# A two-layer hybrid decoder trunk: Strassen pair products with other weight loads, other DMA sums and a written order on every engine

## The chip, the cores and the metric

The kernel runs on one core of one Trainium2 chip. The metric is the device time of one execution in microseconds, as a median over runs. One execution is also profiled; its trace gives the rows that are quoted here. Engines are named as in the profile: PE (TensorE), PEld (its weight loads), DVE (VectorE), ACT (ScalarE), POOL (GpSimd) and SP (SyncE, which here only issues DMAs).

## What is computed

Two layers over a sequence of 1024 tokens of width 1024. Cut to what matters:

```python
for l in range(2):
    shift, scale, gate = split(silu(c) @ w_ada[l] + b_ada[l], 3)
    h = rmsnorm(x, norm_g[l]) * (1 + scale) + shift
    p = h @ w_in[l]                       # 1024 x 9224, split into head groups
    mq, mk, mv, mo, mz, mi, mf, rq, rk, rv, rz = split_cols(p)
    qk = silu(causal_dwconv(concat(mq, mk), conv_w[l], conv_b[l]))      # 4 taps
    cell = mlstm_chunkwise(qk, mv, mi + b_igate[l], mf + b_fgate[l])    # 4 heads x 256
    y_m = sigmoid(mo) * head_layernorm(cell, gn_m[l]) * silu(mz)
    ret = retention_chunkwise(rotary(rq), rotary(rk), rv)               # 4 heads x 256
    y_r = head_layernorm(ret, gn_r[l]) * silu(rz)
    x = x + gate * (concat(y_m, y_r) @ w_out[l])
return rmsnorm(x, final_g)
```

Both head groups are causal linear attentions. The kernel computes them in four chunks of 256 tokens with a running state.

## The kernel before

Every large product is made in three matmuls of float32r pieces (`mm3`, lines 153 to 156): an operand is split into a rounded high part H and the rest L, and HH + HL + LH is summed in PSUM. So each weight tile of 128 x 512 that comes from DRAM is cast by ACT (`wH`) and subtracted by DVE or POOL (`wL = w - wH`, `split_to`, line 758).

**Stages of a layer.** First come the normalised transposed input `hT` and three columns of gates, then `build_forms` (line 570), then the *pair stage* with the projections and the attention, then the output projection (`out_units`). The pair stage is most of the time.

**Pairs.** Two blocks of 128 columns of `w_in` (or two heads' value columns) are multiplied with both halves of the sequence by a Strassen-Winograd scheme: seven products in place of eight. `build_forms` makes the sums of the input (U1 to U4) once per layer, on DVE. `weight_forms` (line 601) makes the seven forms of four weight blocks a11, a12, a21, a22 (a *quad*): a11, a12, a22 and the sums S1 to S4. A job of `pair_units` (line 662) is one quad: seven products of twelve 128x512 matmuls into banks X, Y and Z, where X and Z are added to again after ACT has copied an intermediate sum out of them (`A.copy(keep[n], bank)`, line 674). DVE adds the copies (lines 677 to 684). A job of `vpair_units` (line 690) takes two quads, seven products in two halves (`part`) of 24 matmuls of 256 columns; line 720 is its copy. `plan` (line 1450) lists a layer's 32 jobs: 4 of values (v), 8 of q, 8 of k, 4 of z gates (z) and 8 of a z and an o gate (a).

**The weights before.** Of the seven forms of a quad, a12 and a22 go through `loaded` (line 615): POOL issues a plain load into `wH` (L617), ACT writes its negative into `wL` (L618), and POOL issues an adding DMA of the same block into `wL` (L619). The others start from three tiles that SP loads (`raw`, L607), three adding DMAs of POOL (L623, L632, L633) and one DVE sum (L627), then a cast and a subtraction each (L759, L760). The `Feeder` (line 649) keeps five forms ready (`AHEAD`).

**What follows a product.** `conv_silu` (line 762) is a chain ACT, six small DVE steps, ACT, DVE for the four-tap convolution and its SiLU (L766 to L776); `spill` (line 809) splits the result and stores it to DRAM. `rot_done` does the rotary form, `z_done` and `zo_done` the gates, `store` (line 693) the values. All of a chain is written at the product that it follows.

**Attention.** `attention` (line 862) is a generator that is launched after a head's k job; each `yield n` lets n products pass. Several heads may be under way. It loads q, k, values and key rows back from DRAM, makes scores, state updates and outputs for four chunks, normalises, and stores to `ndr`.

**Order.** PE's instructions stand as written (`manual`, line 1281). The orders of ACT, DVE, POOL and SP are made by a list scheduler from priorities, except in the startup; lines 671 and 717 raise the priority of what follows a product. Each engine, once built, runs its own list strictly in order, and so does SP with its DMAs. Tiles come from tagged pools; a new tile waits until a buffer of its tag is free. Tags here: `acc` (6 buffers), `th` (4), `raw` (5), `wH` and `wL` (5 each), `b` (61).

Of the kernel before, what the change touches and what calls it, by code (L numbers as in the profile page):

```python
# [36 lines left out]
NB = 61  # L37
NACC = 6
NTH = 4
NW = 5  # L40
NRAW = 5
AHEAD = 4
# [47 lines left out]
def tile_hybrid_trunk(ctx, tc, x, xt, c, positions, w_ada, b_ada, norm_g, w_in, w_blk, w_val, conv_w, conv_b,  # L90
# [38 lines left out]
    def launch(gen, delay=0):  # L129
        uid[0] += 1  # L130
        pending.append([clock[0] + delay, uid[0], gen])

    def tick():
        clock[0] += 1
        while True:
            due = [p for p in pending if p[0] <= clock[0]]
            if not due:
                return
            p = min(due, key=lambda q: (q[0], q[1]))
            try:  # L140
                p[0] = clock[0] + next(p[2])
            except StopIteration:
                pending.remove(p)

# [8 lines left out]
    def mm3(o, lt, rt, start, stop, more=False):  # L153
# [29 lines left out]
           for l in range(DEPTH)]  # L183
    mdr = [dpool.tile([NH, T], F32, name=f"mdr{l}") for l in range(DEPTH)]
# [90 lines left out]
    def ada_rows(l, c0, accs):  # L275
        acc = wt("acc", 512, NACC)
        accs.append(acc)
        prev = None
        for k in range(KT + 1):
            raw = None  # L280
            if k < KT:
                raw = wt("acc", 512, NACC)
                Q.dma_start(raw, w_ada[l, k * P:(k + 1) * P, c0:c0 + 512])
            if k == 1:
                V.tensor_scalar(acc, prev, cact[:, 0:1], None, ALU.mult)
            elif k > 1:
                V.scalar_tensor_tensor(acc, prev, cact[:, k - 1:k], acc, ALU.mult, ALU.add)
            prev = raw
            yield 2

    def ada_columns_later(l):
        for half in range(2):
            accs = []
            for which in range(2):
                yield from ada_rows(l, which * D + half * 512, accs)
            yield 2
            pt = ps_a()
            for which in range(2):
                for i in range(4):
                    PE.matmul(pt[:, which * 4 + i:which * 4 + i + 1], accs[which][:, i * P:(i + 1) * P], ones,  # L300
                              start=True, stop=True)
            finish_gsh(l, half * 4, 4, pt[:, 0:4], pt[:, 4:8])
            yield 1

    def gate_rows(l, res):
        for half in range(2):
            accs = []
            yield from ada_rows(l, 2 * D + half * 512, accs)
            brow = wt("th", 512, NTH)
# [5 lines left out]
            a2 = (wt("wH", 512, NW, F32R), wt("wL", 512, NW, F32R))  # L315
# [5 lines left out]
            g = bt()  # L321
            V.tensor_copy(g, pt)
            res.append(g)
# [38 lines left out]
    def load_w_raw(l, c0):  # L362
        for p in range(2):
            raw = wt("raw", 512, NRAW)
            Q.dma_start(raw, w_block(l, c0, p))
            yield raw

    def split_w(raw, eng=G, tiles=None):
        wH, wL = tiles or (wt("wH", 512, NW, F32R), wt("wL", 512, NW, F32R))
        split_to((wH, wL), raw, eng)  # L370
        return [(wH[:, a * P:(a + 1) * P], wL[:, a * P:(a + 1) * P]) for a in range(4)]

    def third(pair, p):
        return [t[:, p * 512:(p + 1) * 512] for t in pair]

    def load_w(l, c0):
        res = []
        for raw in load_w_raw(l, c0):
            res += split_w(raw)
        return res  # L380
# [16 lines left out]
    def rotary_tables():  # L397
        c1, c2, c3 = two_pi_split()
        t0, t1 = wt("q", 1024, 2), wt("kc", 1024, 1)
        ang, turn, tmp, rnd = (t0[:, i * CH:(i + 1) * CH] for i in range(4))  # L400
        a1, pos = (t1[:, i * CH:(i + 1) * CH] for i in range(2))
        a2 = ang
        for n in range(4):
            i, cs = n // 2, slice((n % 2) * CH, (n % 2 + 1) * CH)
            Q.dma_start(pos.bitcast(I32), positions[0:1, n * CH:(n + 1) * CH].to_broadcast([P, CH]))
            yield 2
            V.tensor_copy(ang, pos.bitcast(I32))
            V.tensor_scalar(ang, ang, kc[:, C_FREQ:C_FREQ + 1], None, ALU.mult)
# [4 lines left out]
            V.scalar_tensor_tensor(turn, a2, c2, turn, ALU.mult, ALU.add)  # L413
            for src, cc in ((a1, c2), (a2, c1), (a1, c1)):
# [13 lines left out]
            yield 2  # L428
# [113 lines left out]
    def gate_z(src, g, sign=1.0):  # L542
        th = wt("th", 512, NTH)
        A.activation(th, src, AF.Tanh, scale=0.5 * sign)
        V.scalar_tensor_tensor(g, th, 1.0, src, ALU.add, ALU.mult)

    def gate_o(src, g, store, sign=1.0):
        th = wt("th", 512, NTH)
# [21 lines left out]
    def build_forms(hT):  # L570
        F = {"11": [hT[k][0] for k in range(4)], "21": [hT[k][0] for k in range(4, 8)],
             "22": [hT[k][1] for k in range(4, 8)], "U1": [], "U2": [], "U3": [], "U4": []}
# [11 lines left out]
        for k in range(4):  # L584
# [8 lines left out]
            u4 = whole(hT[k + 4][0])  # L593
            V.scalar_tensor_tensor(u4, u2, -1.0, u4, ALU.mult, ALU.subtract)
            keep("U4", u4)
        return F

    ORDER = (("X", "11"), ("Y", "21"), ("X", "U2"), ("Z", "U1"), ("X", "U3"), ("Z", "22"), ("X", "U4"))
    VORDER = (("Y", "21"), ("X", "11"), ("X", "U2"), ("Z", "U1"), ("X", "U3"), ("Z", "22"), ("X", "U4"))

    def weight_forms(blk, first):
        def tiles():
            return wt("wH", 512, NW, F32R), wt("wL", 512, NW, F32R)

        def raw(src):
            t = wt("raw", 512, NRAW)
            Q.dma_start(t, src)  # L607
            return t

        def split(r, eng):  # L610
            w = tiles()
            split_to(w, r, eng)
            return w

        def loaded(src):
            w = tiles()
            G.dma_start(w[0], src)  # L617
            A.activation(w[1], f(w[0]), AF.Copy, scale=-1.0)  # L618
            G.dma_start(w[1], src, accum_op=ALU.add)  # L619
            return w  # L620

        a, s1, s3 = raw(blk[0][0]), raw(blk[1][0]), raw(blk[0][0])
        G.dma_start(s1, blk[1][1], accum_op=ALU.add)  # L623
        if first == "21":
            yield loaded(blk[0][1])
        w = split(a, G)
        V.tensor_tensor(a, a, s1, ALU.add)  # L627
        yield w
        if first == "11":
            yield loaded(blk[0][1])  # L630
        w = split(a, V)
        G.dma_start(a, blk[0][1], accum_op=ALU.add)  # L632
        G.dma_start(s3, blk[1][0], accum_op=ALU.add)  # L633
        yield w
        yield split(s1, G)
        yield split(s3, V)
        yield split(a, G)
        yield loaded(blk[1][1])

    def pair_forms(l, cols2):  # L640
        for w in weight_forms([[w_block(l, c, kh) for kh in range(2)] for c in cols2], "11"):
            yield [(w[0][:, k * P:(k + 1) * P], w[1][:, k * P:(k + 1) * P]) for k in range(4)]

    def vpair_forms(l, heads):
        gens = [weight_forms([[w_val[l, h, kh * 2 + kp] for kh in range(2)] for h in heads], "21") for kp in range(2)]
        for ws in zip(*gens):
            yield [(w[0][:, a * HD:(a + 1) * HD], w[1][:, a * HD:(a + 1) * HD]) for w in ws for a in range(2)]

    class Feeder:
        def __init__(self, gens):  # L650
            self.gens, self.ready = gens, []
            self.forms = (w for g in gens for w in g())

        def take(self):
            while len(self.ready) <= AHEAD:
                w = next(self.forms, None)
                if w is None:
                    break
                self.ready.append(w)
            return self.ready.pop(0)  # L660

    def pair_units(feed, F, done, loose=False):
        bank, keep = {}, {}
        for n, (b, form) in enumerate(ORDER):
            w = feed.take()
# [24 lines left out]
    def vpair_units(l, feed, F, heads):  # L690
        banks, keeps = [{}, {}], [{}, {}]

        def store(part, i, half, src):
            vH, vL = (wt("acc", 512, NACC, F32R) for _ in range(2))
            A.activation(vH, src, AF.Copy, scale=-1.0 if i else 1.0)
            if i:
                V.scalar_tensor_tensor(vL, src, -1.0, f(vH), ALU.mult, ALU.subtract)
            else:
                V.tensor_tensor(vL, src, f(vH), ALU.subtract)
            dst = vdr[l][heads[i]][half * 2 + part].rearrange("(i t p) c -> i p t c", i=2, p=P)  # L700
# [3 lines left out]
        for n, (b, form) in enumerate(VORDER):  # L704
            w = feed.take()
            for part in range(2):
                bank, keep = banks[part], keeps[part]
# [9 lines left out]
                with tc.high_priority():  # L717
                    if n == 1:
# [3 lines left out]
                        store(part, 0, 0, bank["Y"])  # L722
# [3 lines left out]
                    elif n == 4:  # L726
                        V.tensor_tensor(keep[3], bank["X"], keep[3], ALU.add)
                        store(part, 1, 1, keep[3])
                    elif n == 5:
                        V.tensor_tensor(bank["Z"], bank["Z"], keep[2], ALU.add)  # L730
                        store(part, 0, 1, bank["Z"])
                    elif n == 6:
                        store(part, 1, 0, bank["X"])
                yield

    def z_done(store):
        def done(m, half, src):
            g = wt("acc", 512, NACC)
            gate_z(src, g, -1.0 if m else 1.0)
            Q.dma_start(store[m][half], g)  # L740
        return done

    def zo_done(store):
        g, late = {}, []

        def done(o, half, src):
            if not o:
                g[half] = wt("acc", 512, NACC)
                gate_z(src, g[half])
                if half:  # L750
                    gate_o(late[0], g[1], store[1], -1.0)
            elif half:
                late.append(src)
            else:
                gate_o(src, g[0], store[0], -1.0)
# [6 lines left out]
    def conv_silu(l, hg, which, m, half, pt, halo):  # L762
# [4 lines left out]
        if half == 0:  # L767
            V.tensor_copy(halo, pt[:, HALF - 3:HALF])
        for d in range(1, 4):
# [4 lines left out]
        th = wt("th", 512, NTH)  # L774
        A.activation(th, acc, AF.Tanh, scale=0.5)
        V.scalar_tensor_tensor(acc, th, 1.0, acc, ALU.add, ALU.mult)  # L776
        return acc

    def k_store(src, l, hg, m, half):
        zt = wt("th", 512, NTH)  # L780
# [773 lines left out]
```

## Time and profile before

| what | value |
|---|---|
| median of 2 runs | 2927.63 us (2924.39 to 2930.87) |
| the profiled execution | 2911.5 us |
| its span, first to last instruction | 2909.8 us |
| mean granted TensorE clock | 0.888 |
| busy: PE, DVE, POOL, ACT | 2279.8, 1677.8, 1151.3, 1142.9 us |
| DMA moved | 567.91 MB, mean 195 GB/s |

An engine's busy time is the union of its instructions' spans. Matmuls are pipelined and their spans overlap, so a busy PE is not a PE at its peak; its pace is read from the distances of starts. The granted clock is the share of full clock that PE was given. The DMA share is the mean busy share of the core's 16 DMA engines. In a row of waits, "A <- B" means that A's engine sat idle until B ended; a wait for several things is put down to the one that came last.

### The profile page before, as it was taken

The page shows a single profiled execution, that of the slowest core. Times are in us where ns is not written, and L with a number is a line of the kernel's source. Part 1 is how long each engine was busy: PE and PEld are TensorE (multiplying, and loading weights), DVE is VectorE, ACT ScalarE, POOL GpSimd, SP SyncE. Part 2 cuts the span into 40 slices and gives each one's busy share as a digit, 9 for nine tenths or more (in the row PEclk, how much of TensorE's full clock was granted, in tenths as well). Part 3 has the DMA queues.
Part 4 walks back from the last instruction along what each step waited for, and adds up shares of the span by engine and source line. Part 5 has one row for each costly group of instructions (what it writes and reads, how often), then busy time and mean ns, then how long its engine had stood idle before and what let it go on. Part 6 is the DMA issues. An engine that isn't in the chain of part 4 may idle for free. (4 is left out here: it accounts for less than half of the span.)

```text
span 2909.8 us, 35824 instructions
## 1 busy us (share of the span) xinstructions
PE 2279.8 (78%) x11483; PEld 1931.8 (66%) x11483; DVE 1677.8 (58%) x3073; ACT 1142.9 (39%) x2091; POOL 1151.3 (40%) x1174
## 2 busy tenths in 40 slices
PE   4878787768777767689998788788777776777998
PEld 3668666657565755577776677667766575666777
DVE  4875365655655556656638556456455556574744
ACT  4523233233434344444354333333344434353433
POOL 0533454444434343422266344255343434343123
PEclk7978898888898888799998898889888888898999
DMA  6277787878777877768542787688777787776766
GB/s 212 52 169 199 180 222 199 228 215 240 203 208 186 225 205 186 196 172 275 199 141 62 184 223 210 175 231 230 211 205 184 190 223 184 193 203 171 237 209 170
DMA packets 532553, 567.91 MB, mean 195 GB/s; under 512 B 196466, under 2 KB 347770, under 8 KB 532364
## 3 DMA queue, kind: packets, MB, share of 16 engines
q1 hardware_dynamic: 463676, 440.55, 48.3%
q0 software_dynamic: 68544, 124.81, 24.0%
q8 instruction: 90, 1.47, 0.2%
q14 instruction: 99, 0.81, 0.1%
q10 hardware_dynamic: 144, 0.26, 0.0%
HBM read 409.20 MB, written 156.27 MB: 194 GB/s over the span
## 5 line engine op out<-in xcount | busy, mean ns | idle before, releaser
L154 PE MATMUL pp<-b,wH 128*128 128x512 f32 x1616 | 681.6, 422 | 338.1 <-ACT acc L674 326.0
L156 PE MATMUL pp<-b,wL 128*128 128x512 f32 x1616 | 664.8, 411 | 13.3 <-DMA wL<-in_w_blk_dram 8.0
L155 PE MATMUL pp<-b,wH 128*128 128x512 f32 x1616 | 668.0, 413 | 4.3 <-DVE b L1120 4.3
L154 PEld LDWEIGHTS pp<-b,wH 128*128 128x128 f32 x1616 | 327.1, 202 | 431.2 <-ACT acc L674 351.2
L760 POOL TENSOR_TENSOR wL<-raw,wH 128x512 fp32r<-128x512 f32 x276 | 392.0, 1433 | 405.4 <-ACT wH L759 332.2
L759 ACT CAST wH<-raw 128x512 fp32r<-128x512 f32 x476 | 289.7, 616 | 372.0 <-PE pp L155 129.8
L156 PEld LDWEIGHTS pp<-b,wL 128*128 128x128 f32 x1616 | 326.3, 202 | 90.2 <-DMA wL<-in_w_blk_dram 9.3
L155 PE MATMUL pp<-wL,b 128*128 128x256 f32 (+1 forms) x1024 | 325.2, 318 | 64.5 <-DMA wL<-in_w_val_dram 57.7
L155 PEld LDWEIGHTS pp<-b,wH 128*128 128x128 f32 x1616 | 328.5, 203 | 70.1 <-DVE b L1120 6.5
L154 PE MATMUL pp<-wH,b 128*128 128x256 f32 (+1 forms) x1024 | 325.7, 318 | 55.4 <-ACT acc L720 24.5
L156 PE MATMUL pp<-wH,b 128*128 128x256 f32 (+1 forms) x1024 | 321.8, 314 | 0.2
L155 PEld LDWEIGHTS pp<-wL,b 128*128 128x128 f32 x1024 | 215.3, 210 | 74.3 <-DMA wL<-in_w_val_dram 61.0
L154 PEld LDWEIGHTS pp<-wH,b 128*128 128x128 f32 x1024 | 215.0, 210 | 66.6 <-ACT acc L720 25.8
L618 ACT ACTIVATE wL<-wH 128x512 fp32r<-128x512 f32 x136 | 85.7, 630 | 430.2 <-DMA wH<-in_w_blk_dram 288.8
L760 POOL TENSOR_TENSOR acc<-acc,acc 128x512 fp32r<-128x512 f32 x128 | 179.7, 1420 | 156.4 <-ACT acc L759 126.0
L619 POOL DMA_DIRECT2D wL<-in_w_blk_dram x104 | 92.0, 884 | 343.1 <-ACT wL L618 260.4
L760 DVE TENSOR_TENSOR wL<-raw,wH 128x512 fp32r<-128x512 f32 x200 | 156.7, 785 | 111.6 <-ACT wH L759 111.1
L156 PEld LDWEIGHTS pp<-wH,b 128*128 128x128 f32 x1024 | 214.9, 210 | 7.3 <-DVE b L1120 2.4
L771 DVE SCALAR_TENSOR_TENSOR acc<-pp,cols,acc 128x511 f32<-128x511 f32 (+2 forms) x192 | 142.4, 742 | 33.4 <-ACT acc L766 32.1
L627 DVE TENSOR_TENSOR raw<-raw,raw 128x512 f32<-128x512 f32 x68 | 54.8, 807 | 147.7 <-POOL wL L760 104.2
L759 ACT CAST acc<-acc 128x512 fp32r<-128x512 f32 x128 | 78.4, 617 | 130.7 <-DVE acc L848 48.3
L760 POOL TENSOR_TENSOR sL<-th,sH 128x384 fp32r<-128x384 f32 (+1 forms) x64 | 62.3, 973 | 108.9 <-ACT sH L759 87.8
(342 smaller groups left out, 4393.1 us busy)
## 6 DMA issues: line engine op xcount, KB each, us to landing
raw<-in_w_blk_dram SPq DMA_DIRECT2D x171, 256.0 KB
raw<-in_w_blk_dram POOLq DMA_DIRECT2D x156, 256.0 KB, 5.3
vdr<-acc SPq DMA_DIRECT2D x128, 256.0 KB
ring<-vdr SPq DMA_DIRECT2D x64, 512.0 KB
qdr<-acc SPq DMA_DIRECT2D x128, 256.0 KB
q<-qdr SPq DMA_DIRECT2D x64, 512.0 KB
kfr<-acc SPq DMA_DIRECT2D x128, 256.0 KB
kc<-kfr SPq DMA_DIRECT2D x64, 512.0 KB
```

The costliest lines, as they stand in the source:

```text
L154: PE.matmul(o, lt[0], rt[0], start=start, stop=False, skip_group_check=more)
L155: PE.matmul(o, lt[0], rt[1], start=False, stop=False, skip_group_check=more)
L156: PE.matmul(o, lt[1], rt[0], start=False, stop=stop, skip_group_check=more)
L618: A.activation(w[1], f(w[0]), AF.Copy, scale=-1.0)
L619: G.dma_start(w[1], src, accum_op=ALU.add)
L627: V.tensor_tensor(a, a, s1, ALU.add)
L759: A.copy(dst[0], src)
L760: eng.tensor_tensor(dst[1], src, f(dst[0]), ALU.subtract)
L771: V.scalar_tensor_tensor(acc[:, d:], pt[:, 0:HALF - d], wcol, acc[:, d:], ALU.mult, ALU.add)
```

## The change

- **Weights.** All seven forms of a quad are made alike. SP loads seven tiles from the ring `R` (13 buffers, which replaces `raw` and `wL`); four adding DMAs of POOL make S1 = a21 + a22, S2 = a11 + S1, S4 = a12 + S2 and S3 = a21 + a11, of which S2 and S4 add a tile of SBUF. ACT casts each, and POOL (a12, S3, a22) or DVE (a11, S2, S1, S4) subtracts. `loaded` and the DVE sum go.
- **Times.** The `Feeder` holds a list of events. Each event has the number of the product at which its instruction is written: loads 6 to 11 products ahead of use in a pair job, casts 3, subtractions 2.
- **One-product steps.** Chains are generators whose links stand one product apart.
- **Attention.** One head at a time follows `TABLE`, one entry per product; the next may begin after entry 23. Loading of key rows (`k_load`) and their split (`k_split`) are apart.
- **Order.** From `build_forms` to the last gate pair every engine and the load queue run as written. Outside, the scheduler uses another model of time (`schedule_with_timeline_sim`). Layer 0's plan and layer 1's are reordered. `th` is merged into `acc` (11 buffers); `b` has 59. The sums U4 are made after the others. The gate rows of the second layer go through DRAM (`gbd`).

```diff
-NB = 61
-NACC = 6
-NTH = 4
+NB = 59
+NACC = 11
 NW = 5
-NRAW = 5
-AHEAD = 4
+NR = 13
...
-    def weight_forms(blk, first):
...
-        def loaded(src):
-            w = tiles()
-            G.dma_start(w[0], src)
-            A.activation(w[1], f(w[0]), AF.Copy, scale=-1.0)
-            G.dma_start(w[1], src, accum_op=ALU.add)
-            return w
...
+    def ring_load(src):
+        r = wt("R", 512, NR)
+        Q.dma_start(r, src)
+        return r
+
+    def high(r, h=None):
+        h = wt("wH", 512, NW, F32R) if h is None else h
+        A.copy(h, r)
+        return h
+
+    def low(h, r, eng=G):
+        lo = wt("R", 512, NR, F32R)
+        eng.tensor_tensor(lo, r, f(h), ALU.subtract)
+        return lo
...
+    POOL_LOW = ("a12", "S3", "a22")
...
+        def quad(self, names, blk, t0, u):
+            r, h = {}, {}
+            at = {n: t0 + u * i for i, n in enumerate(names)}
...
+            def add(n, src):
+                G.dma_start(r[n], r[src] if isinstance(src, str) else src, accum_op=ALU.add)
...
+            T2 = at["S2"]
+            ev(T2 - 10, load, "S1", a21)
+            ev(T2 - 8, load, "S2", a11)
+            ev(T2 - 8, add, "S1", a22)
+            ev(T2 - 6, load, "S4", a12)
+            ev(T2 - 6, add, "S2", "S1")
+            ev(T2 - 4, add, "S4", "S2")
+            T4 = at["S3"]
+            ev(T4 - 7, load, "S3", a21)
+            ev(T4 - 5, add, "S3", a11)
+            for n, src in (("a11", a11), ("a12", a12), ("a22", a22)):
+                ev(at[n] - 7 + u, load, n, src)
+            for n in names:
+                ev(at[n] - 4 + u, hi, n)
+                ev(at[n] - 2, lo, n, G if n in POOL_LOW else V)
...
+    def conv_chain(l, hg, which, m, half, pt, halo):
...
         A.activation(acc, pt, AF.Identity, bias=cl[:, 8 + ct:9 + ct], scale=cl[:, 72 + ct:73 + ct])
...
+        yield 1
         for d in range(1, 4):
...
+        yield 1
+        th = wt("acc", 512, NACC)
         A.activation(th, acc, AF.Tanh, scale=0.5)
+        yield 1
         V.scalar_tensor_tensor(acc, th, 1.0, acc, ALU.add, ALU.mult)
+        yield 1
+        yield from spill(acc, l, hg, which, m, half)
...
+    TABLE = ("q0 k0 v0 d0 d1 t0", "", "", "m0", "s0 S0", "k1", "m1 q1", "v1", "V001", "S1 t1", "U01",
+             "k2 q2 d2", "s1 v2", "V10 U2 m2", "S2", "k3 d3", "V11 U3", "t2 q3", "s2 v3", "", "V20 U4 m3", "S3", "",
+             "V21 U5", "", "", "", "V30", "V31", "")
+    RELEASE = 23
...
+        jobs_manual = tc.manual_schedule()
+        jobs_manual.__enter__()
+        launch(build_forms(hT, F))
...
-                    launch(attention(l, h, gt), 4)
+                    launch(attention(l, h, gt), 6, 1)
+        jobs_manual.__exit__(None, None, None)
...
-    with tile.TileContext(nc) as tc:
+    with tile.TileContext(nc, schedule_with_timeline_sim=True) as tc:
```

464 lines of the change are left out of this document (251 added, 213 removed).

## The prediction

> **What bounds it now.** I read the windows by stage first, then who PE waits for, then the timeline of one long wait. The page gives the span; the other rows are busy us (instructions) of PE, PEld, DVE, ACT and POOL, then granted clock, DMA share and GB/s, for pairs, output projection, pairs, output projection of the two layers, and then the same for the attention's PSUM tiles `pa` alone.
>
> ```profile
> span 2909.8 us, 35824 instructions
> ```
>
> ```profile
> 119.00:1306.00 1187.00, 889.80 (x4654) 763.42 (x4653) 711.13 (x1349) 437.86 (x816) 484.22 (x509) 0.87 0.75 198
> 1306.00:1556.00 250.00, 240.18 (x1042) 191.65 (x1043) 130.79 (x197) 113.17 (x184) 106.20 (x84) 0.98 0.59 190
> 1556.00:2706.00 1150.00, 887.25 (x4632) 766.36 (x4630) 661.06 (x1213) 444.09 (x827) 487.10 (x511) 0.87 0.75 196
> 2706.00:2910.00 204.00, 184.45 (x805) 150.13 (x804) 103.80 (x178) 80.04 (x144) 50.82 (x43) 0.96 0.68 205
> ```
>
> ```profile
> 119.00:1306.00 1187.00, 161.05 (x1124) 152.29 (x1124) 75.89 (x187) 35.06 (x77) 0.87 0.75 198
> 1556.00:2706.00 1150.00, 157.85 (x1080) 149.50 (x1080) 75.68 (x182) 36.40 (x79) 0.87 0.75 196
> ```
>
> In the output projections PE is busy 240 of 250 us; in the pair stages 890 of 1187 and 887 of 1150. These two stages are the change's ground. Busy spans overlap, so the pace is read from starts in the timeline:
>
> ```profile
> 706.63 0.39 PE L154 MATMUL pp<-b,wH 128*128 128x512 f32 x1
> 709.35 0.39 PE L154 MATMUL pp<-b,wH 128*128 128x512 f32 x1
> 713.56 0.28 PE L155 MATMUL pa<-q,kc 128*128 128x256 f32 x1
> 713.68 0.28 PE L156 MATMUL pa<-q,kc 128*128 128x256 f32 x1
> ```
>
> The first two rows are twelve matmuls apart, one Strassen product: 2.72 us. A 256-column matmul takes 0.12 us, so half a value product (24 of them) takes 2.88. By the plan a layer has 28 jobs of 7 products and 4 value jobs of 14 halves: 196 x 2.72 + 56 x 2.88 = 694 us. With 1124 and 1080 attention matmuls of 0.12 (135 and 130 us), PE needs 829 and 824 us. It takes 1187 and 1150, so 684 us are lost. The waits of PE (us in total, times, longest) say to whom:
>
> ```profile
> PE pp L154 <- ACT acc L674: 326.0, 54, 17.7
> PE pp L155 <- DMA wL<-in_w_val_dram: 57.7, 15, 8.1
> PE pp L154 <- ACT acc L720: 24.5, 5, 13.3
> PE pp L156 <- DMA wL<-in_w_blk_dram: 8.0, 3, 4.3
> ```
>
> L674 is ACT's copy of bank X, 0.58 us long, after which PE may add to X again. It is late because ACT is one queue, and other work stands ahead of the copy:
>
> ```profile
> 1104.60 0.63 ACT L618 ACTIVATE wL<-wH 128x512 fp32r<-128x512 f32 x1 [4.02 <-DMA wH<-in_w_blk_dram]
> 1109.50 0.63 ACT L775 ACTIVATE th<-acc 128x512 f32<-128x512 f32 x1 [3.08 <-DVE acc L773]
> 1111.46 0.58 ACT L674 COPY acc<-pp 128x512 f32<-128x512 f32 x1
> ```
>
> ```profile
> 1099.08 0.85 POOL L617 DMA_DIRECT2D wH<-in_w_blk_dram  x1
> ```
>
> ```profile
> 1112.09 0.79 PE L154 MATMUL pp<-b,wH 128*128 128x512 f32 x1 [14.00 <-ACT acc L674]
> ```
>
> ACT stood 4.02 us for a weight whose load POOL had issued 5.5 us earlier, and 3.08 us for the convolution on DVE, with the copy behind both; PE stood 14.00 us. Then its matmul took 0.79 us where a warm one takes 0.39. So a wait of this length is paid twice.
>
> [...]
>
> **The change, part by part.** The groups and issues concerned (count | busy us, mean ns | idle before them), then the DMA queues (packets, MB, share of 16 engines) and the landing of POOL's loads to `raw` and to `wL`:
>
> ```profile
> L618 ACT ACTIVATE wL<-wH 128x512 fp32r<-128x512 f32 x136 | 85.7, 630 | 430.2 <-DMA wH<-in_w_blk_dram 288.8 <-DMA wH<-in_w_val_dram 107.0 <-issue 22.1
> L759 ACT CAST wH<-raw 128x512 fp32r<-128x512 f32 x476 | 289.7, 616 | 372.0 <-PE pp L155 129.8 <-DMA raw<-in_w_blk_dram 58.1 <-PE pp L156 43.0
> L760 DVE TENSOR_TENSOR wL<-raw,wH 128x512 fp32r<-128x512 f32 x200 | 156.7, 785 | 111.6 <-ACT wH L759 111.1
> L627 DVE TENSOR_TENSOR raw<-raw,raw 128x512 f32<-128x512 f32 x68 | 54.8, 807 | 147.7 <-POOL wL L760 104.2 <-issue 23.7 <-DMA raw<-in_w_blk_dram 12.3
> L619 POOL DMA_DIRECT2D wL<-in_w_blk_dram x104 | 92.0, 884 | 343.1 <-ACT wL L618 260.4 <-ACT cf L969 36.2 <-ACT b L806 9.4
> L617 POOL DMA_DIRECT2D wH<-in_w_blk_dram x104 | 69.6, 669 | 33.0 <-PE pp L156 30.5 <-issue 2.5
> ```
>
> ```profile
> q1 hardware_dynamic: 463676, 440.55, 48.3%
> q0 software_dynamic: 68544, 124.81, 24.0%
> raw<-in_w_blk_dram POOLq DMA_DIRECT2D x156, 256.0 KB, 5.3
> DMA to landing us min/median/max: 3.7/4.6/8.4
> ```
>
> Work is counted per quad, the seven forms of four weight blocks: 72 of them (28 + 2 x 4 per layer). *ACT:* seven copies of 0.62 to 0.63 us before and after, change 0. What goes is standing in its queue for `wH`, 288.8 + 107.0 = 396 us: a plain load now leaves SP three products (8.2 us) before ACT's copy needs it. *DVE:* two subtractions and one sum (2 x 0.785 + 0.807 = 2.38 us) become four subtractions (3.14): 0.76 x 72 = 55 us more, 27 per layer beside 711. I cost it at nothing, since DVE would be busy (711 + 27) / 1012 = 73% of the stage forecast below; uncovered it is 55 us. *POOL:* seven DMA issues become four, three fewer at 0.67 to 0.88 us, 2.0 to 2.6 us a quad, off the path. *SP:* three loads become seven; one issue takes about 0.4 us:
>
> ```profile
> 1098.99 0.38 SPq L607 DMA_DIRECT2D raw<-in_w_blk_dram  x1
> ```
>
> That is 4 x 72 x 0.38 = 109 us in a queue that holds the stores of `spill`, `store` and `finish` and the attention's loads; nothing, while SP is ahead. *DMA engines:* q0 took 24.0% of 2909.8 us for 124.81 MB, 476 transfers of 256 KB, 1.47 us each; q1 takes 48.3% for 440.55 MB, 0.84 us per 256 KB. Of POOL's seven, two are plain; at 0.84 us these leave (7 x 1.47 - 2 x 0.84) / 5 = 1.72 us for an adding one. Before: 5 x 1.72 + 5 x 0.84 = 12.8 us a quad. After: 4 x 1.72 + 7 x 0.84 = 12.8. If adding costs only 1.47, it is 11.8 against 12.8, 72 us less in all. The two adds whose source lies in SBUF have no row here; if each costs a plain transfer more, 2 x 0.84 x 72 = 121 us come on top. I take 0, by the rows of adds from DRAM, and keep -72 and +121.
>
> *Order.* Where the scheduler ordered ACT, DVE, POOL and SP, each now runs as written, links of a chain one product apart. A link of 0.6 to 0.8 us has 2.72 us to finish before the next engine reaches its successor, so the 3.08 us kind of standing goes too. The moved attention issues per head, on SP, 4 loads each of q, k and values, 12 of key rows and 16 stores, past weight loads written up to ten products ahead. Its last head starts some 22 products before the pair stage ends and its table has 30, so about a quarter of its 135 / 8 = 17 us of PE, 4 us a layer, goes over into the output projection: moved, not added, and taken as 0. The price is that nothing overtakes: behind a late weight ACT holds the bank copies and DVE's chains wait. `build_forms` only spreads; its DVE work stays. `schedule_with_timeline_sim` touches the output projections, idle 250 - 240 + 204 - 184 = 30 us: at best 30 us; at worst they fall to the pair stage's busy share 0.75, 240 / 0.75 - 250 + 184 / 0.75 - 204 = 111 us. I take 0, their own rows.
>
> *Sum.* The pair stages hold 1187 x 0.75 = 890 and 1150 x 0.75 = 863 us of full DMA use, more than PE's 829 and 824, so once ACT's standing is gone the transfers are late next. How dense can they run?
>
> ```profile
> 400.00:700.00 300.00, 226.22 (x1066) 186.61 (x1065) 181.08 (x336) 98.19 (x186) 131.42 (x135) 0.89 0.80 216
> 1910.00:1970.00 60.00, 51.77 (x229) 41.85 (x229) 30.74 (x54) 20.01 (x37) 31.55 (x32) 0.93 0.89 234
> ```
>
> The best 60 us hold 0.89. I take 0.88 for the whole stage: 890 / 0.88 = 1012 and 863 / 0.88 = 980 us, 175 and 170 saved. Against the waits it fits: 345 of the 416 us in the four rows above and their cold clock. The profiled execution took 2911.5 us: 2911.5 - 345 = 2566. The median of the runs shown, 2927.63, is 16 above it, so the forecast is 2582 us. Its own range goes from a share of 0.95 (937 + 908, 492 saved: 2436) to 0.80 (1113 + 1078, 146 saved: 2782), which also holds the DMA bounds (-72 / 0.88 = -82 and +121 / 0.88 = +138: 2500 and 2720).
>
> **Rivals.** *Slower: POOL's chained adds.* S1 must land before S2 adds it, S2 before S4, and S3 after its load, each with two products, 5.44 us. Landing from a POOL issue now has a median of 5.3 us for `raw` and of 4.6 for `wL`, with a maximum of 8.4, at a share of 0.75. While POOL stands, the low parts of three products, of the spills and of the scores wait behind, and then PE. With three such waits a quad, a landing of L costs 72 x 3 x (L - 5.44) us: from L = 7.0 the 345 us are gone; at 7.5, 445 us, 3027. For it: denser DMAs land later. Against: forms are finished one to three products before use.
>
> *Transfers stay at their present best.* If 0.80, the best 300 us, is a ceiling, 2782. For it: 300 us hold nearly half a stage's jobs of every kind. Against: the 0.89 row. [...]
>
> *All stalls go.* DMA at 0.95, PE near 829 / 937 = 88%: 2436.
>
> *The wait only moves.* `acc` has 11 buffers and now serves `th` too, and with a product between links a convolution's tile lives some seven products. ACT's first instruction then waits for a store to land, with the copies behind it: the 326.0 us stay, the 57.7 + 8.0 of DMA waits go, 2862, 2930 if they return elsewhere, and over 2% slower only if the ring starves the casts too. For it: a k job alone fills 8 to 9 buffers. Against: only the 8 k jobs of a layer are such, and 4 of them have no convolution.
>
> **Chances.** Forecast 0.43, all stalls go 0.14, transfers capped 0.15, the wait moves 0.12, POOL's adds 0.16. Faster by over 2% (about what a measurement of this kernel can tell from no change) is 0.43 + 0.14 + 0.15 = 0.72; of the moved wait 0.09 is within 2% and 0.03 slower; slower 0.16 + 0.03 = 0.19. The range runs from 2410, leaving out a little of the all-go case (0.05), to 2915, leaving out POOL's adds (0.15 of 0.16).
>
> **What would show it.** Right: the wait on L674's successor falls from 326 us to under 100; no ACT idle ended by a load of `wH`; pair stages near 1010 and 980 us at a DMA share of 0.88 and a clock over 0.92; output projections as now. Wrong: POOL idle ended by landings of its own adds, with PE waiting for POOL's low parts (first rival); a share stuck at 0.80 with SP or ACT waiting for landings (second); ACT idle ended by landings of stores from `acc` (fourth). What would break the prediction is a longer output projection, or SP standing for a store with weight loads queued behind it: then every engine waits and the DMA share falls below 0.75.

## Result and profile after

The changed kernel takes 2621.97 us (median of 2 runs, 2620.6 to 2623.33) against 2927.63: ratio 0.8956, 95% interval 0.8909 to 0.9003, faster. The forecast was 2582. The profiled execution took 2620.6 us, 291 less than that of before (2911.5).

First the page of the changed kernel: its span, and the rows of the DMA queues (packets, MB, share of 16 engines).

```profile
span 2618.9 us, 35874 instructions
...
q1 hardware_dynamic: 503420, 512.92, 61.7%
q0 software_dynamic: 39168, 71.32, 16.2%
```

Then the windows by stage, cut at the same places in PE's program as before: pairs and output projection of the first layer, then of the second (busy us and instructions of PE, PEld, DVE, ACT, POOL; granted clock, DMA share, GB/s).

```profile
117.00:1106.00 989.00, 853.40 (x4628) 739.30 (x4627) 743.98 (x1374) 417.11 (x808) 429.18 (x415) 0.93 0.88 248
1106.00:1404.00 298.00, 258.64 (x1091) 205.22 (x1089) 141.60 (x224) 124.23 (x201) 107.51 (x81) 0.91 0.46 153
1404.00:2398.00 994.00, 858.83 (x4634) 741.93 (x4632) 695.82 (x1270) 425.70 (x822) 433.67 (x420) 0.93 0.85 239
2398.00:2619.00 221.00, 188.26 (x782) 150.84 (x780) 102.05 (x164) 77.19 (x138) 49.88 (x41) 0.93 0.65 191
```

For a fair difference the kernel before is cut at the same places in its program, by the trace at 119, 1302, 1561 and 2706 us:

```profile
119.00:1302.00 1183.00, 889.68 (x4654) 763.42 (x4653) 708.69 (x1346) 435.89 (x813) 483.21 (x508) 0.87 0.75 198
1302.00:1561.00 259.00, 245.30 (x1065) 195.79 (x1065) 137.38 (x205) 119.54 (x195) 111.26 (x87) 0.97 0.58 187
1561.00:2706.00 1145.00, 882.25 (x4610) 762.22 (x4608) 656.91 (x1207) 439.68 (x820) 483.05 (x510) 0.87 0.76 197
2706.00:2910.00 204.00, 184.45 (x805) 150.13 (x804) 103.80 (x178) 80.04 (x144) 50.82 (x43) 0.96 0.68 205
```

The two pair stages lost 194 and 151 us, together 345; the two output projections gained 39 and 17, together 56; the startup lost 2. That is the whole difference of 291. Who PE waits for in the changed kernel (us, times, longest):

```profile
PE pa L1082 <- DVE cL L1055: 75.7, 37, 5.4
PE pp L155 <- ACT wH L381: 58.8, 8, 21.1
PE pp L155 <- ACT acc L716: 32.9, 17, 5.3
PE pp L155 <- ACT b L1213: 29.3, 6, 8.8
```

L716 is the old L674, the copy of bank X: 326.0 us have become 32.9. ACT now comes to this copy early: 73 of its 156 times it stood ready until PE's product ended (142.3 us in all), before 9 times (9.8 us). New at the top is the low part `cL` of the attention's state, which DVE makes one product behind ACT's high part. POOL does stand for the landings of what its adds need:

```profile
POOL R L661 <- DMA R<-in_w_blk_dram: 135.5, 40, 11.7
POOL R L661 <- DMA R<-R: 59.3, 18, 6.1
```

### The profile page after: what moved, and what is told of

It reads as the page before. It is cut to its first block, busy times and chain, and to the rows that moved or that the text cites. A ratio compares the mean times of both kernels' runs of the same rounds, so it can differ in the third digit from the quotient of the medians.

```text
span 2618.9 us, 35874 instructions
## 1 busy us (share of the span) xinstructions
PE 2239.9 (86%) x11483; PEld 1898.4 (72%) x11483; DVE 1752.9 (67%) x3165; ACT 1110.6 (42%) x2087; POOL 1041.1 (40%) x978
## 3 DMA queue, kind: packets, MB, share of 16 engines
q1 hardware_dynamic: 503420, 512.92, 61.7%
q0 software_dynamic: 39168, 71.32, 16.2%
## 5 line engine op out<-in xcount | busy, mean ns | idle before, releaser
L155 PE MATMUL pp<-b,wH 128*128 128x512 f32 x1616 | 660.9, 409 | 72.6 <-ACT acc L716 32.9
L157 PE MATMUL pp<-b,R 128*128 128x512 f32 x1616 | 658.7, 408 | 39.0 <-POOL R L386 28.7
L386 POOL TENSOR_TENSOR R<-R,wH 128x512 fp32r<-128x512 f32 x276 | 410.9, 1495 | 314.5 <-ACT wH L381 286.7
L381 ACT CAST wH<-R 128x512 fp32r<-128x512 f32 x616 | 373.1, 617 | 360.7 <-DMA R<-in_w_blk_dram 78.6
L155 PEld LDWEIGHTS pp<-b,wH 128*128 128x128 f32 x1616 | 320.1, 198 | 146.7 <-ACT acc L716 42.3
L157 PEld LDWEIGHTS pp<-b,R 128*128 128x128 f32 x1616 | 318.2, 197 | 126.1 <-POOL R L386 39.6
L386 DVE TENSOR_TENSOR R<-R,wH 128x512 fp32r<-128x512 f32 x340 | 269.9, 801 | 141.4 <-ACT wH L381 134.6
L156 PE MATMUL pp<-R,b 128*128 128x256 f32 (+1 forms) x1024 | 319.6, 312 | 27.4 <-POOL R L386 24.3
L156 PEld LDWEIGHTS pp<-R,b 128*128 128x128 f32 x1024 | 208.2, 203 | 38.6 <-POOL R L386 27.1
L661 POOL DMA_DIRECT2D R<-R x136 | 121.3, 898 | 247.2 <-DMA R<-in_w_blk_dram 88.0
L716 ACT COPY acc<-pp 128x512 f32<-128x512 f32 x156 | 91.4, 586 | 150.7 <-PE pp L157 142.3
L661 POOL DMA_DIRECT2D R<-in_w_blk_dram x104 | 100.8, 969 | 82.1 <-DMA R<-in_w_blk_dram 47.5
```

The lines of the kernel that those rows point to most:

```text
L155: PE.matmul(o, lt[0], rt[0], start=start, stop=False, skip_group_check=more)
L156: PE.matmul(o, lt[0], rt[1], start=False, stop=False, skip_group_check=more)
L157: PE.matmul(o, lt[1], rt[0], start=False, stop=stop, skip_group_check=more)
L381: A.copy(h, r)
L386: eng.tensor_tensor(lo, r, f(h), ALU.subtract)
L661: G.dma_start(r[n], r[src] if isinstance(src, str) else src, accum_op=ALU.add)
```

## Experiments

All ratios are against the kernel before on the same chip, with their 95% intervals. The median of that kernel was 2912.79 to 2918.31 us there. So the changed kernel's gain of 0.1044 is about 305 us, and 0.01 is 29 us.

The change has three parts that can be separated: the code of the pair stage (weight loads, chained sums, one-product links, longer rings, the attention's table, the jobs in another order), the order on ACT, DVE, POOL and SP in that stage, and the scheduler's model of time. The table puts the medians together; each run follows.

| code | order in the pair stage | time model | us | ratio |
|---|---|---|---|---|
| before | scheduler | no | 2916 | 1 |
| before | scheduler | yes | 2799.94 | 0.9605 |
| changed | scheduler | no | 2737.21 | 0.9387 |
| changed | as written | no | 2650.19 | 0.9082 |
| **changed** | **as written** | **yes** | **2621.97** | **0.8956** |
| changed | written, but SP by scheduler | yes | 2608.91 | 0.8947 |
| changed | SP written, the rest by scheduler | yes | 2505.80 | 0.8592 |
| changed | scheduler | yes | 2456.06 | 0.8404 |

### The time model taken out of the changed kernel

```diff
-    with tile.TileContext(nc, schedule_with_timeline_sim=True) as tc:
+    with tile.TileContext(nc) as tc:
```

> The changed kernel with the scheduler's old model of time, which orders only what lies outside the written stretch. The two output projections grew from 259 and 204 to 298 and 221 us, 56 us together. If the other model of time is what made them longer, they come back to about 259 and 204 and the time falls by about 50 us, to near 2570; the pair stages stay at 989 and 994. If the merged rings and the late end of the attention made them longer, the time stays within 10 us of 2622.

2650.19 us, ratio 0.9082 (0.9064 to 0.91): neither 2570 nor 2622. So the model does not lengthen the output projections; it helps by 28 us in the medians. In the spans (2650.3 against 2618.9) 13 us of it lie in the startup, and 11 in the two projections, which take 305 and 225 us without it (298 and 221 with it).

### The scheduler's order in the changed kernel

```diff
-        jobs_manual = tc.manual_schedule()
-        jobs_manual.__enter__()
...
-        jobs_manual.__exit__(None, None, None)
```

> The changed kernel with the written stretch given back to the scheduler (PE stays as written). If the plain loads and sums carry the gain, the time stays within 2% of 2622. If the order carries it, the pair stages go back to 1100 us or more each and the time to 2850 or more.

2456.06 us, ratio 0.8404 (0.8367 to 0.844): 166 us faster than the changed kernel, with the same instructions on PE in the same order. Neither theory had it. Windows of its pair stages, then its PE waits:

```profile
105.00:1030.00 925.00, 832.83 (x4629) 726.80 (x4628) 752.36 (x1382) 432.48 (x814) 432.32 (x410) 0.96 0.92 261
...
1307.00:2217.00 910.00, 831.97 (x4630) 724.43 (x4629) 709.71 (x1267) 431.91 (x824) 435.38 (x414) 0.96 0.91 257
```

```profile
PE pp L155 <- ACT acc L716: 47.7, 25, 4.8
PE pp L155 <- ACT b L1213: 26.4, 6, 6.8
```

The wait on `cL` is gone from the list, and the wait on L716 stays short. The written order is thus not what ended the 326 us, and it costs time. The clock gives some of it: for the same matmuls PE is busy 832.83 and 831.97 us, where it was 853.40 and 858.83, at a clock of 0.96 in place of 0.93. How the clock follows a wait is seen in the kernel before: after the wait of 14.00 us on L674 that the prediction quotes, the granted clock is 0.50 from 1112.09 to 1116.40 us, and matmuls of 512 columns take 0.79 and 0.63 us; from 1116.60 to 1119.90 it is 1.00, and they take 0.39. In its pair stages the kernel with the higher clock and 47 us less of PE busy time has 97 waits of 170 us in all, against 130 waits of 270 us in the changed kernel; that the fewer waits gave it the clock was not tried by itself.

### The time model in the kernel before, and the changed code without it

The first run puts `schedule_with_timeline_sim=True` into the kernel before, and changes nothing else.

> The kernel before, with nothing changed but the scheduler's time model for the four engines other than PE. Theory A, the kernel's own parts carry the gain (plain loads, chained sums, links one product apart, two long buffer rings): the time model is worth about what it was worth in the changed kernel, 28 us there, so 2860 to 2920 against 2916. Rival B, most of the 460 us between the kernel before and the changed kernel in the scheduler's order come from the time model's order: 2550 to 2750, with the wait of PE on the copy of bank X (L674, 326 us before) under 150 us.

2799.94 us, ratio 0.9605 (0.9575 to 0.9636). The wait on L674 hardly moved:

```profile
PE pp L154 <- ACT acc L674: 312.3, 44, 14.4
```

The second run is the changed code in the scheduler's order, without the model.

> The changed kernel in the scheduler's order (2456 us with the time model), now without the time model. Theory A: the kernel's own parts carry the gain, and the model adds some 28 us: 2460 to 2500. Rival B, the model's order is what makes it fast: 2580 to 2800, with long waits on the copy of bank X (L716, 48 us with the model) again.

2737.21 us, ratio 0.9387 (0.9359 to 0.9414). Its waits and pair stages:

```profile
PE pp L157 <- DVE R L386: 113.2, 38, 7.3
PE pp L155 <- ACT acc L716: 51.1, 30, 5.0
```

```profile
119.00:1169.00 1050.00, 874.25 (x4631) 750.57 (x4629) 734.57 (x1381) 427.49 (x810) 429.25 (x409) 0.91 0.81 229
1463.00:2506.00 1043.00, 867.41 (x4632) 745.41 (x4631) 698.49 (x1269) 438.05 (x827) 427.86 (x414) 0.92 0.81 225
```

Both theories fell in part. The code alone brings 0.0613, about 179 us, and with it alone the wait on the bank copy is short. The model alone brings 0.0395, 115 us. Together they bring 0.1596, 465 us, far more than the sum of 294. Without the model the scheduler lets DVE make the low parts of weights too late (113.2 us); with it, and with the written order, that row is some 10 us or less.

So the change's own gain divides as follows, if one steps from kernel to kernel in this order (in another order the parts come out otherwise: the model alone is worth 115 us with the old code): code 0.0613 (179 us), written order in place of the old scheduler's 0.9387 - 0.9082 = 0.0305 (89 us), time model outside the written stretch 0.9082 - 0.8956 = 0.0126 (37 us by the ratios, 28 by the medians).

### Which queue pays for the written order

```diff
-        jobs_manual = tc.manual_schedule()
+        ENG = mybir.EngineType
+        jobs_manual = tc.manual_schedule(engines={ENG.Activation, ENG.DVE, ENG.Pool})
```

> The changed kernel with the written order kept on ACT, DVE and POOL and taken off SP's queue alone in the stretch from the forms to the last gate pair. Theory A, the 166 us that the written order costs come from SP, where weight loads stand behind stores that wait for DVE, ACT and POOL (43, 40, 38, 34 and 32 us in the largest rows of SP's waits), so that ACT's casts and POOL's adds wait for landings: 2450 to 2520. Rival B, they come from ACT, DVE and POOL standing in line for each other (ACT's copy of L716 stood 142 us for PE, POOL's low parts 287 us for ACT's casts, PE 76 us for DVE's low part of the state): 2590 to 2630.

```diff
-        jobs_manual = tc.manual_schedule()
+        jobs_manual = tc.manual_schedule(engines={mybir.EngineType.SP})
```

> The counterpart: SP's queue alone in written order, ACT, DVE and POOL in the scheduler's. Theory A, SP's queue costs the 166 us: 2590 to 2640. Rival B, the compute engines' order costs them: 2450 to 2520, with PE's wait on DVE's low part of the state (75.7 us now) under 20 us. If both this run and the one before lie between 2520 and 2590, each queue bears a part.

SP freed: 2608.91 us, ratio 0.8947 (0.8923 to 0.8972), 13 us by the medians and nothing that the ratio's interval can tell from the changed kernel. ACT, DVE and POOL freed: 2505.80, ratio 0.8592 (0.8565 to 0.8618), 116 us, and PE's wait on `cL` is gone from its list. The compute engines' order bears the larger part of the 166 us. SP's matters by some 50 us once theirs is free (2505.80 to 2456.06). What SP's written order does is seen at the start of the pair stages: in the kernel with SP written, whose rows stand below, the first value product waits 24.8 us for its first weights in the first layer and 21.8 in the second, together most of the 50; in the kernel with all four free the whole row is 6.4 us.

```profile
PE pp L155 <- ACT acc L716: 65.2, 32, 6.2
PE pp L155 <- ACT wH L381: 59.4, 10, 24.8
```

### One link of a chain undone

```diff
             A.copy(new[0][:, :, 0:W], cf[:, :, 0:W])
-            yield 1
             V.tensor_tensor(new[1][:, :, 0:W], cf[:, :, 0:W], f(new[0][:, :, 0:W]), ALU.subtract)
```

> The changed kernel in its written order, with one link undone: DVE's low part of the attention's state (cL, L1055) is written into the same product as ACT's high part (cH, L1053) and no longer one product behind it. PE waits 75.7 us, 37 times, for that low part, the largest row of PE's waits. Theory A, the one-product link is part of what the written order costs: that wait falls under 25 us, and the time by 50 to 110 us (the wait and the clock after it), to 2510 to 2570. Rival B, the wait only moves (DVE now stands for ACT with its other links behind it): 2600 to 2640.

2596.17 us, ratio 0.8898 (0.887 to 0.8926): 17 us by the ratios, 26 by the medians, below what the first theory named and just outside the second's range. Who waited for the low part (now L1054), and the first rows of PE's waits:

```profile
  PE pa L1081: 5.7, 6
```

```profile
PE pp L155 <- ACT wH L381: 58.5, 8, 21.7
PE pa L155 <- ACT n L1137: 36.8, 11, 9.5
PE pp L155 <- ACT acc L716: 32.1, 18, 4.9
```

The 75.7 us fell to 5.7, and 17 to 26 us of these 70 reached the time. Some of it came back as other waits: the row of `n` was 21.8 us in the changed kernel and is 36.8 here. A link that stands one product behind its forerunner is part of the price of the written order, but a small one; no single row holds the 116 us.

### Plain loads alone, in the kernel before

```diff
-            w = tiles()
-            G.dma_start(w[0], src)
-            A.activation(w[1], f(w[0]), AF.Copy, scale=-1.0)
-            G.dma_start(w[1], src, accum_op=ALU.add)
-            return w
+            return split(raw(src), G)
```

To fit, `b` has 60 buffers and `raw` 6, and the tile of S3 is loaded after S2 is made. The scheduler and its lack of a time model are those of before.

> The kernel before, in the scheduler's order, with the forms a12 and a22 loaded plainly by SP, cast by ACT and subtracted by POOL (one more raw buffer, one fewer b; S3's load stands later). If ACT's standing for POOL's loads was the main cause, most of the 396 us of ACT idle goes, PE's wait on the copy of X falls from 326 us to under 170, and the time falls by 150 to 250 us, to 2680 to 2780. If the order was the cause, ACT stands as long for other things, and the time stays within 2% of 2928.

2798.16 us, ratio 0.9589 (0.9559 to 0.9619), between what the two theories named. PE's first wait, then ACT's rows for weights:

```profile
PE pp L154 <- ACT acc L671: 299.0, 48, 17.1
```

```profile
ACT wH L756 <- PE pp L155: 213.3, 129, 5.5
...
ACT wH L756 <- DMA raw<-in_w_blk_dram: 106.4, 40, 7.7
```

ACT's 396 us of standing for `wH` are gone, and 106.4 us for `raw` stand in their place (58.1 before). The wait on the copy (L671 here) is 299.0 us: it lost 27. ACT standing for those loads was therefore not the main cause of that wait. The trace of the kernel before already says so when ACT's timeline is laid over PE's 54 waits on L674: of the 326 us ACT worked 149 on what stood ahead of the copy, stood 108 for DVE and 31 for loads of `wH`, and the rest for POOL, other loads and issue. Most of the 396 us of standing fell where PE was not waiting for the copy. Standing shortly before such a wait can delay the copy too, but taking all of it away moved only these 27 us. The gain of 4% came with the end of PE's waits on `wL` from DRAM (57.7 + 8.0 us before) and of the adding transfers of `loaded`; how it divides was not measured.

### POOL's loads put back into the changed kernel

```diff
-            for n, src in (("a11", a11), ("a12", a12), ("a22", a22)):
-                ev(at[n] - 7 + u, load, n, src)
...
+            ev(at["a11"] - 7 + u, load, "a11", a11)
+            for n, src in (("a12", a12), ("a22", a22)):
+                ev(at[n] - 8 + u, pool_load, n, src)
+                ev(at[n] - 5 + u, negative, n)
+                ev(at[n] - 4 + u, add_low, n, src)
```

`pool_load`, `negative` and `add_low` are the three steps of the old `loaded`. `NW` is 7 and `NR` 11; the order is written.

> The changed kernel in its written order, with a12 and a22 made as before: a plain load by POOL into wH, ACT's negative, and an adding DMA of POOL (7 buffers of wH, 11 of R). ACT reaches the negative three products after the load, so it should stand little. Per quad that is 6 adding and 7 plain transfers in place of 4 and 7: 2 x 1.72 x 72 = 248 us more of full DMA use. If the transfers bound the pair stages at a share near 0.88, the time grows by about 280 us, to 2900. If PE's waits on other engines bound them, it grows by less than 60 us. If the way of loading by itself is what cost the time, ACT stands for wH again and PE for the copy of X by more than 150 us.

2735.09 us, ratio 0.9371 (0.9348 to 0.9394), 113 us slower than the changed kernel by the medians. PE's waits and the pair stages:

```profile
PE pp L156 <- DMA R<-in_w_val_dram: 102.1, 25, 17.6
PE pp L157 <- DMA R<-in_w_blk_dram: 73.8, 34, 6.0
...
PE pp L155 <- ACT acc L731: 41.7, 12, 9.4
```

```profile
116.00:1189.00 1073.00, 884.80 (x4629) 761.06 (x4627) 713.33 (x1375) 421.09 (x810) 434.40 (x483) 0.90 0.91 246
1478.00:2521.00 1043.00, 863.40 (x4632) 744.41 (x4631) 668.83 (x1272) 428.97 (x824) 443.18 (x488) 0.91 0.93 245
```

None of the three theories had it. PE's wait on the copy (L731 here) stays near 42 us, so this way of loading does not by itself bring that wait back. But with three products between load and negative ACT stands only 16.1 and 13.9 us for these loads, so the run does not tell what long standing would do. The price is PE waiting for the adding transfers themselves, 102.1 and 73.8 us: the low part is the last thing to land before use. Here the share does reach 0.91 and 0.93; whether the transfers are the limit at this share was not tried.

### One adding transfer less: are the transfers the bound?

```diff
-            ev(T2 - 4, add, "S4", "S2")
```

In the changed kernel:

> The changed kernel in its written order with one adding transfer fewer per quad: form S4 is left as block a12 alone, without S2, so the output is another. Theory A, the pair stages are bound by the transfers at the share of 0.88 that they show, as the forecast had it: 72 x 1.72 / 0.88 = 141 us less, 2480. Rival B, the written order bounds them and the transfers have room: at most 40 us less, 2582 to 2622. Between them, near 2560: what goes is POOL's standing for the landing of this add's source (59 us in the row of R<-R), not the volume.

In the changed code with the scheduler's order and the time model:

> The same transfer left out (form S4 is block a12 alone) in the changed kernel with the scheduler's order and time model (2456 us, DMA share 0.92 and 0.91 in the pair stages). Theory A, there the transfers are the bound: 72 x 1.72 / 0.92 = 135 us less, 2320. Rival B, PE's own 832 busy us of 925 and short waits are: at most 40 us less, 2416 to 2456.

2584.45 us, ratio 0.8869 (0.8838 to 0.89), and 2418.59 us, ratio 0.8301 (0.8269 to 0.8332): by the medians 38 and 37 us less, by the ratios 25 and 30, each against its own kernel. The windows of the first, then of the second:

```profile
115.00:1099.00 984.00, 854.08 (x4631) 740.45 (x4629) 743.60 (x1374) 419.26 (x810) 398.87 (x381) 0.93 0.83 241
1395.00:2363.00 968.00, 849.55 (x4635) 736.84 (x4634) 684.97 (x1270) 425.74 (x823) 406.54 (x386) 0.94 0.82 237
```

```profile
106.00:1021.00 915.00, 829.28 (x4631) 724.83 (x4629) 737.01 (x1381) 429.86 (x814) 403.00 (x378) 0.96 0.88 255
1299.00:2197.00 898.00, 827.95 (x4632) 723.84 (x4631) 695.04 (x1267) 431.31 (x824) 410.26 (x383) 0.96 0.87 251
```

In the changed kernel the transfers of the pair stages fall from 989 x 0.88 + 994 x 0.85 = 1715 us of full use to 984 x 0.83 + 968 x 0.82 = 1611, 104 less, and the stages get only 31 us shorter: the share falls, not the time. A stage at its ceiling would have kept its share. In the scheduler's order full use falls from 925 x 0.92 + 910 x 0.91 = 1679 us to 915 x 0.88 + 898 x 0.87 = 1586, 93 less, and the stages get 22 us shorter. In neither kernel do the transfers alone set the time.

### S4 added by POOL in SBUF

```diff
-            ev(T2 - 4, add, "S4", "S2")
+            ev(T2 - 4, lambda: G.tensor_tensor(r["S4"], r["S4"], r["S2"], ALU.add))
```

> The changed kernel in the scheduler's order with the sum S4 = a12 + S2 made by a POOL addition in SBUF instead of an adding transfer; nothing is left out. POOL gets 72 x 1.45 = 104 us of work and loses 72 issues of 0.91 us, 65 us. Theory A, transfers are the bound in that kernel: 2320 to 2370, the best so far. Rival B, they are not: 2440 to 2480. Rival C, POOL, whose low parts PE needs, becomes late: over 2480, with PE waiting for R of L386 by POOL over 60 us.

This too is in the scheduler's order with the time model. 2448.67 us, ratio 0.8401 (0.837 to 0.8431): no difference from 0.8404. With the run before it, the second theory stands. This kernel and the one with the adding transfer are the fastest that leave nothing out, 16% under the kernel before.

## Why the prediction came out near

**The saving in the pair stages was right in size and wrong in cause.** The sum gave 175 + 170 = 345 us; 194 + 151 = 345 were measured (354 with the stages of before cut as in the prediction). But it took them from "the transfers are late next", at a share of 0.88. The changed kernel does show 0.88 and 0.85, and yet the same transfers run at 0.92 and 0.91 in the scheduler's order, 166 us sooner in all, and taking 104 us of them away saves 31 in the stages. The share was a result of the stage's length, not its limit. That the number fits is chance.

**The main cause named, ACT standing for `wH`, did not carry the wait on L674.** The kernel before without `loaded` still waits 299.0 us of 326.0 there, and by the trace only 31 of the 396 us fell inside these waits. In two more runs of the table ACT's standing for weights and PE's wait on the copy do not go together. With the time model in the kernel before, ACT's standing for `wH` falls by half (first two rows, against 288.8 and 107.0) and PE waits 312.3 us for the copy; with the changed code in the scheduler's order without the model, ACT stands long for weights again (last two rows), and PE waits 51.1 us:

```profile
ACT wL L618 <- DMA wH<-in_w_blk_dram: 122.1, 67, 5.6
ACT wL L618 <- DMA wH<-in_w_val_dram: 66.8, 27, 7.0
...
ACT wH L381 <- DMA R<-in_w_blk_dram: 173.0, 51, 10.1
ACT wH L381 <- DMA R<-R: 48.1, 18, 5.5
```

With the changed code PE's wait on the copy is short in every order (32.9, 47.7, 51.1, 65.2 us). So the rest of the code ended it: the one-product links, the chained sums, the rings of 11 and 13, the attention's table, or the new order of the jobs. No run takes these apart. The traces point at the links: inside PE's waits on the copy ACT stood 108 us for DVE in the kernel before, 99 without `loaded`, 6 with the changed code in the scheduler's order without the model, and 1 in the changed kernel. That the links did this is argued, not shown. The one timeline of a wait that the prediction quoted had both kinds of standing in it, and I took the one with the larger total in ACT's waits as the cause.

**"Order" was half right.** That links one product apart end ACT's standing for DVE fits the figures just given. Against the scheduler without a time model, as in the kernel before, the written order wins 87 us by the medians (2737.21 to 2650.19) and 89 by the ratios. Against the scheduler with the model it loses 166. The price named there, that nothing overtakes, is real: 116 us on ACT, DVE and POOL, with SP second at some 50 once theirs are free.

**The time model was taken as an affair of the output projections.** In the change that is nearly so, since the pair stage is written: 28 us, half of it in the startup. In the scheduler's hands it is worth 115 us with the old code and some 280 with the new.

**The output projections were taken at 0 and cost 56 us**, within the -30 to +111 named. With the 2 us won in the startup this is the whole difference between the sum, 2566, and the measured 2620.6. They are longer with the changed code in every order: 295 and 225 us in the scheduler's order without the model, 276 and 217 with it, against 259 and 204. So the code by itself lengthens them; with the model, the written order adds 26 of the 56 us (519 against 493). In the first of them there are 26 matmuls more than before (1091 against 1065), some 3 us, as the prediction's step about the table said; in the second there are 23 fewer (782 against 805), and it is 17 us longer all the same. The rest shows in waits of PE, mostly for the split inputs (L1213 and L1214), 64 us in the two stages against 25 before, and in a lower clock (0.91 against 0.97, 0.93 against 0.96). Why these inputs come later was not tried.

**The transfers' sum held, the number of quads did not.** From the queue's rows an adding transfer now takes 0.162 x 2618.9 / 272 = 1.56 us and a 256 KB on the other queue 0.83, so a quad takes 4 x 1.56 + 7 x 0.83 = 12.0 us, where I took 12.8 for both. The 272 are 71.32 MB at 256 KB, four for each of 68 quads. The 72 of the prediction was a miscount of the plan: it has six a jobs a layer and 30 jobs in all, not eight and 32, so 26 jobs and 4 value jobs, and the x136 and x68 of the quoted rows said 68. With 182 x 2.72 + 56 x 2.88 + 135 PE needs 791 us for the first layer, not 829, so the stages lost more than the 684 us named; the terms per quad shrink by a twentieth, and the sum, built on shares, does not change.

**The rivals.** POOL's chained adds: its sign is there, 135.5, 59.3 and 42.3 us (the last for value blocks) of POOL's idle time ended by landings before an add, but PE's waits on POOL's low parts are 28.7 and 24.3 us in their two rows, so the finished forms were early enough. Its premise that denser transfers land later holds here: POOL's adds from blocks of `w_in` landed in a median of 5.3 us at shares of 0.75 and 0.76 (`raw`, before) and of 6.7 us at 0.88 and 0.85 (`R`, changed). Transfers capped at 0.80: refuted by 0.88 and 0.92. All stalls go, 2436: not in the changed kernel, but the scheduler's order of the same code comes to 2456, and at a share of 0.92, not 0.95. The wait that only moves into `acc`: no row of ACT's longest waits in the changed kernel ends with a store from `acc`. Of the signs named, the short wait on L716, no ACT idle from a load of `wH`, stages near 1010 and 980 us, and a clock over 0.92 (0.93 in both) came true; none of them could tell the bound by transfers from the bound by order.

## What to carry over

A busy share that rises to a plausible ceiling does not show a bound: take some of that work away and see whether the time or the share falls. A total of idle time in an engine's queue is a cause of another engine's wait only as far as removing it moves that wait, and here it did not. Before such a total is used as a cost, lay the one engine's timeline over the other's waits and count what falls inside. When an order is written by hand, compare it with the best order that the scheduler can make of the same code, not only with the old one.

## What was not expected of the hardware

The transfers took nearly the same engine time in two orders that differ by 166 us. The rows below are those of the changed kernel's code in the scheduler's order (span 2433.7 us): 83.1% of it is 2022 us of full use. In the changed kernel 61.7% + 16.2% of 2618.9 us is 2040, for the same bytes, 0.9% more.

```profile
q1 hardware_dynamic: 503420, 512.92, 65.8%
q0 software_dynamic: 39168, 71.32, 17.3%
```

In the pair stages alone, full use is 1715 us in the changed kernel and 1679 in the scheduler's order. Most of these 2% are bytes, since some transfers fall on the other side of the cut: 989 x 248 + 994 x 239 us x GB/s is 483 MB, 925 x 261 + 910 x 257 is 475. So a share times a length was here a fair measure of the transfers' work, to about 1%. It was no measure of what limits the time.
